# Output projection: the last block goes through DRAM and is split in its turn, x's rows and norm vectors load later, last attention normalisation on VectorE

## The chip, the cores and the metric

The kernel runs on one core of one Trainium2 chip. The metric is the device time of one execution in microseconds (us), as the median of several runs. A profile of one execution, with every engine's instructions, is read beside it. The engines are TensorE (PE; its weight loads are PEld), VectorE (DVE), ScalarE (ACT), GpSimd (POOL) and SyncE (SP), whose queue issues all the transfers of this kernel.

## The reference, cut to what matters

One decoder layer on x of 1024 positions by 1024 columns, all in float32. Four heads of differential attention (`o`, RMS-normalised per head) and a gated short convolution give two halves of 512 columns; they are put together and multiplied by `w_out`; then comes a layer norm over x plus that product, and a gated feed-forward with a second layer norm.

```python
o = o * lax.rsqrt(jnp.mean(jnp.square(o), axis=-1, keepdims=True) + RMS_EPS)
o = o * attn_norm_g.astype(jnp.float32) * (1.0 - lam_init)
...
conv_out = gate_b * causal_dwconv(gate_c * hc, conv_w)
cat = jnp.concatenate([attn_out, conv_out], axis=-1)
return jnp.einsum('bsc,cd->bsd', cat, w_out)
...
h = layer_norm(DEEPNORM_ALPHA * h + mix, ln1_g[l], ln1_b[l])
```

## The kernel before, in words

Every float32 product is made of three TensorE products of operands that are split in two parts, `hi` and `lo` (line 62, `split`: ScalarE copies the rounded part at line 65, VectorE subtracts it at line 66; `mm3`, lines 71 to 76, multiplies hi by hi, hi by lo, lo by hi).

Attention runs head after head, with the projections of the convolution's channel blocks between the heads (`CONV`). The last of these is `conv_3(2)`: `project` ends in a PSUM bank, `convolve(3)` (lines 467 to 473) makes three VectorE passes over 1024 positions, and `gate_out(3, ...)` multiplies the two halves by the gate at line 477, c0 (positions 0 to 511) first. The products of attention and convolution lie in DRAM as eight blocks of 128 channels, two halves of 512 positions each (`cat_d[k][half]`); blocks 0 to 3 are the heads, 4 to 7 the convolution. One piece is the exception: block 7, half 0, is not stored, but split out of `ws[3]` in SBUF, in a tile `c0_7` that is the first tile taken from the ring `e0` (seven tiles; lines 525 to 527). In the profile its two instructions are named `c<-w`.

The normalisation of an attention block (`normalise`, line 357) squares the block, sums it on TensorE against a matrix of ones (`mq`), takes the power on ScalarE (lines 368 to 371), and then does five steps of 128x256 on GpSimd (lines 372 to 376) and a store (line 377). The very last one, of head 3 and positions 768 to 1023, is called at line 519, behind all of attention and convolution.

The output projection goes over eight row tiles `t` of 128 positions; for each it sums over the eight blocks in `K_ORDER = (4, 5, 0, 1, 2, 6, 7, 3)`, position `i`. Rows 0 and 1 are made together: for each `i`, `weights(i)` loads and splits a row block of `w_out` (`wo`), `mixer(i, 0)` loads half 0 of a block (`cr`, four buffers) and splits it into a ring tile (`c<-cr`), and `mms(0, i)`, `mms(1, i)` make 12 matmuls (named `op`). At `i == 5` the loads of x's rows for tiles 0 and 1 (`rows`, tied behind the last `cr` load so far by `after`) and of the two norm vectors g1 and b1 are put in. Row tiles 2 to 7 follow with `norm` of earlier tiles and transposes (`trp`) between their matmuls.

The order of the instructions on each engine is the scheduler's: by the order in the code among what it holds to be ready. On the chip each engine's queue, and SP's queue of transfers, runs in that order and waits at its head.

Of the kernel before, what the change touches and what calls it, by code (L numbers as in the profile page):

```python
# [9 lines left out]
F32R = mybir.dt.float32r  # L10
BF16 = mybir.dt.bfloat16
AF = mybir.ActivationFunctionType
ALU = mybir.AluOpType
# [3 lines left out]
P = 128  # L17
S = 1024
D = 1024
NT = S // P  # L20
NK = D // P
H = 4
# [6 lines left out]
QC = 256  # L29
# [14 lines left out]
def layer_kernel(ctx: ExitStack, tc: tile.TileContext, x, xt, w_in, w_v, lam, vecs, w_out, ln, w_up, w_down, out):  # L44
    nc = tc.nc
    V, A, T, G = nc.vector, nc.scalar, nc.tensor, nc.gpsimd
    SQ = nc.sync
# [6 lines left out]
    def pool(name, stack=None, side=None, space=None, **kw):  # L54
        args = dict(name=name, bufs=1, reuse_waits="tile")
        if space is not None:
            args["space"] = space
        if side is not None:
            args["side"] = side
        return (stack or ctx).enter_context(tc.tile_pool(**args))  # L60

    def split(hi, lo, src, scale=None, eng=None):

        if scale is None:
            A.copy(hi, src)  # L65
            (eng or V).tensor_tensor(lo, src, hi.bitcast(F32), op=ALU.subtract)  # L66
        else:
            A.mul(hi, src, scale)
            V.scalar_tensor_tensor(lo, src, scale, hi.bitcast(F32), op0=ALU.mult, op1=ALU.subtract)
# [24 lines left out]
    RING = [6]  # L94
# [54 lines left out]
    cat_d = [[dram.tile([P, 512], F32, name=f"cat_d{k}_{c}") for c in range(2)] for k in range(8)]  # L149
# [156 lines left out]
    gm = const.tile([P, 1], F32, name="gm")  # L306
    V.tensor_scalar(gm, cols[:, 100:101], -0.5 * (1.0 - LAM_INIT), None, op0=ALU.mult)
    gp = const.tile([P, 1], F32, name="gp")
# [38 lines left out]
    c0, c1 = slice(0, 512), slice(512, 1024)  # L347
# [9 lines left out]
    def normalise(h, c, osb):  # L357
        sq = at.tile([P, QC], F32, name="sq", tag="sq")
        V.tensor_tensor(sq, osb, osb, op=ALU.mult)
        sqh = at.tile([P, QC], F32R, name="sqh", tag="sqh")  # L360
        sql = at.tile([P, QC], F32R, name="sql", tag="sql")
        split(sqh, sql, sq)
        mq = p_pv.tile([P, 512], F32, name="mq", tag="pv", bufs=1)
        T.matmul(mq[:, :QC], ones, sqh, start=True, stop=False)
        T.matmul(mq[:, :QC], ones, sql, start=False, stop=True)

        me = at.tile([P, QC], F32, name="me", tag="sq")
        A.activation(me, mq[:, :QC], AF.Identity, bias=epsc)
        y = at.tile([P, QC], F32, name="y", tag="sql")
        A.activation(y, me, AF.Ln)  # L370
        A.activation(y, y, AF.Exp, scale=-0.5)
        G.tensor_tensor(me, me, y, op=ALU.mult)
        G.tensor_tensor(me, me, y, op=ALU.mult)
        G.tensor_scalar(me, me, gm, gp, op0=ALU.mult, op1=ALU.add)
        G.tensor_tensor(y, y, me, op=ALU.mult)
        G.tensor_tensor(osb, y, osb, op=ALU.mult)
        SQ.dma_start(cat_d[h][c // 2][:, c % 2 * QC:(c % 2 + 1) * QC], osb)

    def attention(h):
# [28 lines left out]
        def spread(c, qi, pm, pa):  # L408
            i, nkb = 2 * c + qi, 2 * c + 2
            for j0 in range(0, i + 1, 4):  # L410
                nj = min(4, i + 1 - j0)
                tp = p_tr.tile([P, 4, P], F32, name="tp", tag="tr", bufs=1)
                for j in range(nj):
                    T.transpose(tp[:, j, :], pm[0][:, (j0 + j) * P:(j0 + j + 1) * P], ident)
                g = pa[j0 // 4]
                split(g[:, 0, 0:nj, qi * P:(qi + 1) * P], g[:, 1, 0:nj, qi * P:(qi + 1) * P], tp[:, :nj, :])
            if qi == 0:
                return
            o = p_pv.tile([P, 512], F32, name="o", tag="pv", bufs=1)
            for j in range(nkb):  # L420
                qs = slice(P if j == nkb - 1 else 0, QC)
                mm3(o[:, qs], vh[:, j, :], vl[:, j, :], pa[j // 4][:, 0, j % 4, qs], pa[j // 4][:, 1, j % 4, qs],
                    j == 0, j == nkb - 1, skip_group_check=True)
            osb = at.tile([P, QC], F32, name="osb", tag="osb")
            A.copy(osb, o[:, :QC])
            rms.append(lambda: normalise(h, c, osb))
# [48 lines left out]
    def gate_out(j, halves):  # L475
        for cs, v in halves:
            V.tensor_tensor(ws[j][:, cs], v, ws[j][:, cs], op=ALU.mult)
            if j < 3 or cs is c1:
                SQ.dma_start(cat_d[4 + j][cs.start // 512], ws[j][:, cs])

    us, ws = {}, {}

# [12 lines left out]
    def conv_2(j):  # L495

        ua, ub = new_u(j + 1)
        _, _, ba, bb = project(16 + j + 1, 12 + j, ua, ub)
        gate_out(j, ((c1, bb), (c0, ba)))

    def conv_3(j):

        va, vb, ba, bb = project(20 + j + 1, 12 + j + 1)
        ca, cb = us[j + 1][:, 2:514], us[j + 1][:, 514:S + 2]
        V.tensor_tensor(ca, va, ca, op=ALU.mult)
        V.tensor_tensor(cb, vb, cb, op=ALU.mult)
        convolve(j + 1)
        gate_out(j + 1, ((c0, ba), (c1, bb)))
# [14 lines left out]
    RING[0] = 7  # L523
    p8_st, hop_st, cp_st, d_st = ExitStack(), ExitStack(), ExitStack(), ExitStack()
    e0 = pool("e0", p8_st)
    cat = {(0, 7): e0.tile([P, 2, 512], F32R, name="c0_7", tag="ring", bufs=RING[0])}
    split(cat[0, 7][:, 0], cat[0, 7][:, 1], ws[3][:, c0])
    ab.close()
    p8 = pool("p8", p8_st, space=PSUM)
    ew = pool("ew", p8_st, side="right")  # L530
# [2 lines left out]
    gp = pool("gp", d_st)  # L533
# [19 lines left out]
    def bcast_row(pl, i, name):  # L553
        tl = pl.tile([P, D], F32, name=name, tag=name)
        SQ.dma_start(tl, ln[i:i + 1, :].broadcast_to([P, D]))
        return tl
# [30 lines left out]
    def weights(i):  # L587
        k = K_ORDER[i]
        raw = wtile([P, 2, 512], f"wo{k}_r")
        SQ.dma_start(raw, w_out[k * P:(k + 1) * P, :].rearrange("p (a b) -> p a b", a=2))  # L590
        w = late_p[i // 2].tile([P, 4, 512], F32R, name=f"wo{k}", tag=f"hb_{LATE_OPS[i // 2]}{'hl'[i % 2]}")
        split(w[:, 0:2], w[:, 2:4], raw)
        wo[k] = w

    def mixer(i, half):
        k = K_ORDER[i]
        if (half, k) in cat:
            return
        cr = cc.tile([P, 512], F32, name="cr", tag="cr", bufs=4)
        last_load[0] = SQ.dma_start(cr, cat_d[k][half])  # L600
        if i < NK - 1:
            c = e0.tile([P, 2, 512], F32R, name=f"c{half}_{k}", tag="ring", bufs=RING[0])
        else:
            c = cx.tile([P, 2, 512], F32R, name=f"c{half}_{k}", tag="c8")
        split(c[:, 0], c[:, 1], cr)
        cat[half, k] = c
# [3 lines left out]
    def rows(t):  # L610
        xr[t] = cx.tile([P, D], F32, name=f"xr{t}", tag="xr", bufs=5)
        d = SQ.dma_start(xr[t], x[t * P:(t + 1) * P, :])
        if t < 2:
            after(d, last_load[0])
# [4 lines left out]
    def mms(t, i):  # L619
        k = K_ORDER[i]  # L620
        c, w, ts = cat[t // 4, k], wo[k], slice(t % 4 * P, (t % 4 + 1) * P)
        for d in range(2):
            mm3(acc[t][d], c[:, 0, ts], c[:, 1, ts], w[:, d], w[:, 2 + d], i == 0, i == NK - 1)
# [61 lines left out]
    for i in range(NK):  # L685
        then.setdefault((3, i), []).append(lambda i=i: mixer(i, 1))
# [5 lines left out]
    for i in range(NK):  # L692
        weights(i)
        mixer(i, 0)
        if i == 5:
            for t in range(2):
                rows(t)
            g1, b1 = bcast_row(cp, 0, "g1"), bcast_row(cp, 1, "b1")
        for t in range(2):
            mms(t, i)  # L700
# [73 lines left out]
    def operand(src, which, i, tail=False, eng=None):  # L774
        if tail and not (which == "T" and i < HK - NTAIL + RT):
            v = ep.tile([P, 2, 512], F32R, name=f"{which}{i}", tag="ra", bufs=NF - NKEEP)
        else:
            v = e0.tile([P, 2, 512], F32R, name=f"{which}{i}", tag="ring", bufs=RING[0])
        split(v[:, 0, :], v[:, 1, :], src, eng=eng)
        return v  # L780
# [124 lines left out]
    def add(x_, y_, op, out=None):  # L905
        if out is None:
            out = ep.tile([P, 512], F32, name="tm", tag="r", bufs=4)
        V.tensor_tensor(out, x_, y_, op=op)
        return out
# [33 lines left out]
    for j in range(HK + 2):  # L943
        if j < HK:
            op = ready.pop(0) if ready else (operand(a11[j], "S", j), operand(b11[j], "T", j))
            for t in range(4):
                mm_row(X, op, t, j == 0, j == HK - 1)
        if j >= 2:
            i = j - 2
            op = (operand(add(a21[i], a22[i], ALU.add), "S", i),  # L950
                  operand(add(b12[i], b11[i], ALU.subtract), "T", i))
# [91 lines left out]
```

## Time and profile before

| | us |
|---|---|
| median of 3 runs (1127.42 to 1127.8) | 1127.51 |
| the profiled execution | 1126.14 |
| its span | 1124.4 |
| PE busy in the span | 1084.9 (96%) |
| DVE busy | 890.2 (79%) |
| ACT busy | 505.3 (45%) |
| POOL busy | 104.7 (9%) |

The span is the time from the first to the last instruction; the execution's own time lies 1.7 us above it. Busy shares are averages over stages with different limits, so the stage around the change, from 355 to 415 us, is read by itself.

### The profile page before, as it was taken

Reading aid. Unit: us, or ns where it says so; the run is one execution under the profiler, and the core shown is the slowest. Engines: PE = TensorE matmul, PEld = TensorE weight load, DVE = VectorE, ACT = ScalarE, POOL = GpSimd, SP = SyncE. Lnnn points to the kernel's source line nnn. Section 1 sums busy time; section 2 is a strip of 40 time slices with the busy share of each in tenths; the row PEclk is TensorE's granted clock in tenths of the full one; section 3 lists DMA queues with packets and bytes.
Section 4 is the critical chain, followed back from the end, with each engine's and each line's share of the span. In section 5 each row is a group of like instructions: output and inputs, shape, how many; then the busy total and the mean of one; then the engine's idle time right before and its main releaser. Section 6 shows DMA issues by size and latency. Waiting matters only on the chain.

```text
span 1124.4 us, 13769 instructions
## 1 busy us (share of the span) xinstructions
PE 1084.9 (96%) x4988; PEld 877.9 (78%) x4988; DVE 890.2 (79%) x1375; ACT 505.3 (45%) x936; POOL 104.7 (9%) x152
## 2 busy tenths in 40 slices
PE   7998999999999699999999999999999999999997
PEld 6877777877768588888888888888888887788885
DVE  7677799689787667898867677777777599997797
ACT  6367586387676311254333333343333343444550
POOL 0002214014032211100000000000000000000102
PEclk9999999999999899999999999999999999999998
DMA  7531201301214537022222222131312295111111
GB/s 268 151 94 43 77 33 48 113 28 48 80 48 147 210 135 272 38 90 98 87 101 75 94 71 99 60 109 57 113 57 94 85 380 219 38 66 38 42 71 76
DMA packets 48404, 113.80 MB, mean 101 GB/s; under 512 B 4816, under 2 KB 15184, under 8 KB 48336
## 3 DMA queue, kind: packets, MB, share of 16 engines
q1 hardware_dynamic: 48336, 112.92, 29.0%
q8 instruction: 39, 0.64, 0.2%
q14 instruction: 29, 0.24, 0.1%
HBM read 86.43 MB, written 26.48 MB: 100 GB/s over the span
## 4 chain that ended last, share of the span: by engine, by line
PE 76%; DVE 12%; ACT 5%; DMA 3%; POOL 2%; issue 2%; SPq 0%; POOLq 0%; DVEq 0%; ACTq 0%
PE X L74 9%; PE X L76 9%; PE X L75 9%; PE Z L76 5%; PE Z L74 5%; PE Z L75 5%; PE op L76 3%; PE op L74 3%; PE op L75 3%; PE dx L75 2%; PE dx L76 2%; PE dx L74 2%; PE Y L76 2%; PE dz L76 2%; PE dz L75 2%; PE Y L74 2%
## 5 line engine op out<-in xcount | busy, mean ns | idle before, releaser
L66 DVE TENSOR_TENSOR a<-s,a 128x512 fp32r<-128x512 f32 x118 | 85.4, 725 | 50.5 <-ACT a L65 49.6
L65 ACT CAST a<-s 128x512 fp32r<-128x512 f32 x118 | 73.6, 624 | 99.9 <-PE X L76 45.7
L65 ACT CAST a<-w 128x512 fp32r<-128x512 f32 x106 | 65.9, 623 | 97.2 <-PE X L76 40.8
L66 DVE TENSOR_TENSOR a<-w,a 128x512 fp32r<-128x512 f32 x106 | 74.1, 701 | 18.2 <-ACT a L65 17.9
L65 ACT CAST T<-b 128x512 fp32r<-128x512 f32 x66 | 40.6, 621 | 68.4 <-PE dz L76 34.0
L75 PE MATMUL dx<-T,S 128*128 128x512 f32 x176 | 69.1, 392 | 1.1 <-DVE T L66 1.1
L76 PE MATMUL dx<-T,S 128*128 128x512 f32 x176 | 68.6, 389 | 0.0
L74 PE MATMUL dx<-T,S 128*128 128x512 f32 x176 | 66.0, 390 | 0.0
L74 PE MATMUL op<-wo,c 128*128 128x512 f32 x128 | 51.5, 402 | 9.1 <-ACT c L65 9.1
L66 DVE TENSOR_TENSOR T<-b,T 128x512 fp32r<-128x512 f32 x66 | 46.0, 700 | 16.6 <-ACT T L65 16.4
L450 DVE TENSOR_REDUCE nm<-sc 128x1 f32<-128x128 f32 (+5 forms) x64 | 47.6, 751 | 6.2 <-PE sc L449 5.7
L75 PE MATMUL dz<-T,S 128*128 128x512 f32 x132 | 51.8, 393 | 0.0
L76 PE MATMUL dz<-T,S 128*128 128x512 f32 x132 | 51.4, 390 | 0.0
L76 PE MATMUL op<-wo,c 128*128 128x512 f32 x128 | 50.8, 397 | 0.2 <-DVE c L66 0.2
L75 PE MATMUL op<-wo,c 128*128 128x512 f32 x128 | 50.6, 396 | 0.0
L454 ACT ACTIVATE p<-sc,nm 128x128 f32<-128x128 f32 (+5 forms) x64 | 47.6, 745 | 6.2 <-DVE p L463 3.8
L74 PE MATMUL dz<-T,S 128*128 128x512 f32 x132 | 48.4, 394 | 0.5 <-ACT T L65 0.4
L813 ACT ACTIVATE t<-t 128x1024 f32<-128x1024 f32 x22 | 23.4, 1062 | 50.3 <-DVE t L812 50.3
L447 PE MATMUL sc<-k,q 128*128 128x512 f32 (+2 forms) x96 | 37.1, 394 | 5.6 <-ACT p L454 4.6
L75 PEld LDWEIGHTS dx<-T,S 128*128 128x128 f32 x176 | 33.0, 188 | 9.7 <-DVE T L66 2.9
L793 POOL MEMSET gs<- 128x2 f32 x22 | 2.2, 99 | 403.0 <-DVE t L812 403.0
L66 DVE TENSOR_TENSOR S<-ra,S 128x512 fp32r<-128x512 f32 x56 | 38.9, 698 | 0.0
(315 smaller groups left out, 3263.2 us busy)
## 6 DMA issues: line engine op xcount, KB each, us to landing
w<-in_w_up SPq DMA_DIRECT2D x44, 512.0 KB, 3.4
b<-in_w_down SPq DMA_DIRECT2D x44, 256.0 KB, 6.8
w<-in_w_in SPq DMA_DIRECT2D x20, 512.0 KB, 3.6
act_d<-act SPq DMA_DIRECT2D x19, 512.0 KB, 2.6
ra<-act_d SPq DMA_DIRECT2D x19, 512.0 KB, 7.5
v_d<-vs SPq DMA_DIRECT2D x16, 256.0 KB, 2.7
vhl<-v_d SPq DMA_DIRECT2D x8, 512.0 KB, 4.6
wo_r<-in_w_out SPq DMA_DIRECT2D x8, 512.0 KB, 3.9
```

The lines of the kernel that those rows point to most:

```text
L65: A.copy(hi, src)
L66: (eng or V).tensor_tensor(lo, src, hi.bitcast(F32), op=ALU.subtract)
L74: T.matmul(ps, lh, rh, start=first, stop=False, **kw)
L75: T.matmul(ps, lh, rl, start=False, stop=False, **kw)
L76: T.matmul(ps, ll, rh, start=False, stop=last, **kw)
L447: T.matmul(sc[:, bs], q2[m][:, qs], k2[m][:, bs], start=True, stop=False)
L450: V.tensor_reduce(nm[:, m:m + 1], sc[:, :n], axis=AX.X, op=ALU.max, negate=True)
L454: A.activation(pt[:, :n], sc[:, :n], AF.Exp, bias=nm[:, m:m + 1], accum_out=sm[:, m:m + 1])
L793: G.memset(gs[:, 0:2], 0.0)
L813: A.activation(t_, t_, AF.Silu)
```

## The change

Three edits. The last normalisation (head 3, last 256 positions) does its five steps on VectorE instead of GpSimd; the other fifteen stay. Half 0 of block 7 is stored to DRAM like all other pieces, and `c0_7` with its early split goes: `mixer(6, 0)` now loads the piece and splits it in its turn. The loads of x's rows 0 and 1 and of g1 and b1 are put in at `i == NK - 1` (7) instead of 5, so that the `after` of the rows refers to the load of block 3, the last one of half 0.

```diff
-        G.tensor_tensor(me, me, y, op=ALU.mult)
-        G.tensor_tensor(me, me, y, op=ALU.mult)
-        G.tensor_scalar(me, me, gm, gp, op0=ALU.mult, op1=ALU.add)
-        G.tensor_tensor(y, y, me, op=ALU.mult)
-        G.tensor_tensor(osb, y, osb, op=ALU.mult)
+        E = V if (h, c) == (H - 1, S // QC - 1) else G
+        E.tensor_tensor(me, me, y, op=ALU.mult)
+        E.tensor_tensor(me, me, y, op=ALU.mult)
+        E.tensor_scalar(me, me, gm, gp, op0=ALU.mult, op1=ALU.add)
+        E.tensor_tensor(y, y, me, op=ALU.mult)
+        E.tensor_tensor(osb, y, osb, op=ALU.mult)
...
-            if j < 3 or cs is c1:
-                SQ.dma_start(cat_d[4 + j][cs.start // 512], ws[j][:, cs])
+            SQ.dma_start(cat_d[4 + j][cs.start // 512], ws[j][:, cs])
...
-    cat = {(0, 7): e0.tile([P, 2, 512], F32R, name="c0_7", tag="ring", bufs=RING[0])}
-    split(cat[0, 7][:, 0], cat[0, 7][:, 1], ws[3][:, c0])
+    cat = {}
...
-        if (half, k) in cat:
-            return
...
-        if i == 5:
+        if i == NK - 1:
             for t in range(2):
                 rows(t)
             g1, b1 = bcast_row(cp, 0, "g1"), bcast_row(cp, 1, "b1")
```

## Rows read from the trace of the kernel before

**Rows 1.** Waits of PE, whole execution (us in total, times, longest).

```profile
PE op L74 <- ACT c L65: 9.1, 1, 9.1
```

**Rows 2.** Waits of PE from 385 us to the end.

```profile
PE dx L75 <- DVE T L66: 1.1, 2, 0.9
PE dz L74 <- ACT T L65: 0.4, 1, 0.4
```

**Rows 3.** Timeline of PE around the stage (start, us, engine, line, operation).

```profile
370.52 0.28 PE L365 MATMUL mq<-sql,ones 128*128 128x256 f32 x1
379.90 0.79 PE L74 MATMUL op<-wo,c 128*128 128x512 f32 x1 [9.10 <-ACT c L65]
...
384.44 0.39 PE L74 MATMUL op<-wo,c 128*128 128x512 f32 x1
...
385.83 0.40 PE L74 MATMUL op<-wo,c 128*128 128x512 f32 x1
...
412.45 1.03 PE L574 MATMUL trp<-ident,xr 128*128 128x128 f32 x8
```

**Rows 4.** Busy time by stretch: length, PE, PEld, DVE, ACT, POOL, PEclk, DMA share, GB/s.

```profile
380.00:385.00 5.00, 4.83 (x12) 3.35 (x13) 3.04 (x5) 1.41 (x3) 0.08 (x1) 0.56 0.78 199
```

**Rows 5.** Timeline of ACT from 360 us.

```profile
372.16 0.42 ACT L371 ACTIVATE y<-y 128x256 f32<-128x256 f32 x1
378.71 0.62 ACT L65 CAST c<-w 128x512 fp32r<-128x512 f32 x1 [6.13 <-DVE w L477]
379.23 2.17 ACT L65 CAST c<-cr 128x512 fp32r<-128x512 f32 x4
```

**Rows 6.** Timeline of SP, the transfer queue, from 318 us.

```profile
339.95 1.35 SPq L600 DMA_DIRECT2D cr<-cat_d  x3
...
381.46 0.91 SPq L600 DMA_DIRECT2D cr<-cat_d  x2
382.41 0.99 SPq L612 DMA_DIRECT2D xr<-in_x  x2
```

**Rows 7.** Landing of all 15 loads of `cr`, then of `xr`, 375 to 405.

```profile
DMA to landing us min/median/max: 2.7/4.3/8.8
...
DMA to landing us min/median/max: 4.7/8.0/9.8
```

**Rows 8.** Timeline of DVE from 318 us.

```profile
357.68 0.69 DVE L66 TENSOR_TENSOR a<-w,a 128x512 fp32r<-128x512 f32 x1 [1.99 <-ACT a L65]
...
372.13 1.22 DVE L66 TENSOR_TENSOR wo<-wo_r,wo 128x1024 fp32r<-128x1024 f32 x1
...
374.94 1.74 DVE L66 TENSOR_TENSOR wo<-wo_r,wo 128x1024 fp32r<-128x1024 f32 x1
...
377.98 0.69 DVE L477 TENSOR_TENSOR w<-X,w 128x512 f32<-128x512 f32 x1
378.59 0.91 DVE L477 TENSOR_TENSOR w<-p,w 128x512 f32<-128x512 f32 x1
...
380.56 2.49 DVE L66 TENSOR_TENSOR c<-cr,c 128x512 fp32r<-128x512 f32 x4
...
407.96 1.27 DVE L569 SCALAR_TENSOR_TENSOR xr<-xr,rs,b 128x1024 f32<-128x1024 f32 x1
```

**Rows 9.** Transfers, 360 to 400 us, then 325 to 360: count, KB, us to landing.

```profile
cat_d<-w SPq DMA_DIRECT2D x1, 256.0 KB, 2.2
...
cat_d<-w SPq DMA_DIRECT2D x2, 256.0 KB, 4.9
```

**Rows 10.** Instructions of lines 471 and 359 (count, min/median/max ns, first and last start).

```profile
L471 DVE SCALAR_TENSOR_TENSOR w<-u,cols,w x4: 1271/1462/1751, 126.7 to 373.3; 128x1024 f32<-128x1024 f32 x4
L359 DVE TENSOR_TENSOR sq<-osb x16: 416/422/426, 89.9 to 354.3; 128x256 f32<-128x256 f32 x16
```

**Rows 11.** PE by stretch around its wait of 3.50 us (PE, PEclk, DMA share, GB/s).

```profile
104.00:106.00 2.00, 1.27 (x4) 0.64 0.05 18
106.00:108.00 2.00, 2.00 (x7) 0.51 0.00 0
```

## The prediction

> **What bounds the kernel now.** I read the waits of PE first. Over the whole execution the longest is one wait of 9.1 us of the first matmul of the output projection, for ScalarE's copy `c` [rows 1]; it is the stage that the change touches. From 385 us on PE waits for only 1.1 + 0.4 = 1.5 us in 739 [rows 2], so PE sets the time there, and what is saved before that point should reach the end in full.
>
> The timeline of PE shows the price of this stall. The last matmul before it starts at 370.52; its pair started 0.12 earlier, so PE could go on at about 370.7. The first `op` starts at 379.90, and after that PE runs slowly: from 379.90 to 384.44 are nine steps in 4.54 us, later six steps take 384.44 to 385.83, 0.23 each [rows 3]. Nine steps at 0.23 would be 2.1. So 2.4 us more are lost, and the granted clock says to what: 0.56 over 380 to 385, the lower of the two levels (1.2 GHz of 2.4) for most of it [rows 4]. The stage costs 9.1 + 2.4 = 11.5 us in all.
>
> Then the releaser. ScalarE is done with the last normalisation at 372.6, then idles 6.13 us for the convolution's gate (line 477) before `c<-w`, the split of block 7 out of SBUF; the four `c<-cr` come right behind [rows 5]. These four had been loaded long before: SP issued the first three of their loads from 339.95 to 341.3 [rows 6], and no `cr` load of the execution took over 8.8 us [rows 7]. Their data was there, and they stood behind one copy. PE's first matmul needs one of these four (block 4), not block 7, which it wants only at `i` = 6. The eight splits of `wo` ran before `c<-w` although the code asks for them later, so the order was not the code's alone. I infer that the ring gives its tiles in the order asked, and that `c0_7`, which asks first, holds the four.
>
> **The change part by part.** *The early split goes.* The ring's first tile is then block 4's. It lies where operands of the finished projection lay, so the four splits can go as soon as ScalarE and VectorE have room: VectorE waited 1.99 us before 357.68 alone [rows 8], and a split's lower half costs it 2.49 / 4 = 0.62. PE has `wo` and `c` of the first blocks when it is done with `mq`, and starts at 370.7: it gains 9.1. As it does not pause, it gains the 2.4 of the slow clock too. Were the splits done only in VectorE's full stretch behind 361 us, they would still be ahead of what PE asks: one `wo` and one `c` are 1.22 + 0.62 = 1.84 us of VectorE [rows 8] against 12 matmuls, 2.8 us of PE. With their buffers free early, the loads of blocks 2 and 6, which SP issued only at 381.46 [rows 6], leave early too.
>
> *Block 7 through DRAM.* This adds a store, a load and a later split. Call D the end of the first gate product of line 477; before it is 378.6 [rows 8]. PE asks for block 7 after six positions, 72 matmuls: 370.7 + 72 x 0.231 = 387.3. Behind D come 0.1 for the issue, the store's landing, which SP's queue must wait for, the load's landing, and 0.6 for ScalarE's half of the split; the lower half ends 0.7 later and is wanted 0.46 later, so 0.8 in all. The store took 2.2 us beside other transfers in this stage and 4.9 earlier [rows 9]; the load from 2.7 to 8.8, in the middle 4.3 [rows 7]. I take 2.2, since it was measured in this place, and 4.3, since g1 and b1 (512 KB each) will be in flight with it as g1 and the rows were before.
>
> *The last normalisation on VectorE.* Five steps of the size of line 359, 0.42 each at most [rows 10], add up to 2.1 us on VectorE, and may stand ahead of the gate product or behind it. In return GpSimd no longer disturbs VectorE there: the `wo` split at 374.94 took 1.74 against 1.22 [rows 8], line 471 took 1.75 against 1.27 [rows 10]; D falls by 0.5 + 0.5 = 1.0 to 377.6. If the five steps and the lower halves of blocks 2 and 6 (1.2) all come ahead, D is 380.9. I take 379.0, about half. Block 7 is then ready for PE at 379.0 + 0.1 + 2.2 + 4.3 + 0.8 = 386.4, which is 0.9 before it is wanted: hidden, cost 0. The bounds: at best 377.6 + 0.1 + 2.2 + 2.7 + 0.8 = 383.4, at worst 380.9 + 0.1 + 4.9 + 8.8 + 0.8 = 395.5, a wait of 8.2 us. The store of the normalised block stands in SP's queue ahead of the two stores of `w`; it can hold them up by the five steps at most, which D's upper bound has.
>
> A rule speaks against a round trip like this one. The Trainium skill, DMA: Bandwidth & Descriptors, section Anatomy of one DMA, gives each transfer about 2.0 us that don't shrink with its size, plus its bytes at 436 GB/s (fitted on transfers that GpSimd issues); an estimate from it is 2.6 us for 256 KB, 5.2 for store and load. The rows say 2.2 + 4.3 = 6.5 for the same two. By the page block 7 would come 1.3 us earlier than by the rows and the sum would be the same; the upper rows, 4.9 + 8.8, are what it leaves out, and they carry the second rival.
>
> *Rows of x and norm vectors later.* Four loads of 512 KB are moved, all in SP's queue, from behind block 6's load to behind block 3's. g1 and b1 may slip ahead again, as nothing ties them; the 4.3 above has them in flight. The two rows are issued behind block 3's load, some 0.5 us after block 7's, near 382.5, where the rows were issued before as well (382.41) [rows 6]. Loads of rows landed in 8.0 us in the middle and 9.8 at most [rows 7]: 390.5 to 392.3. Tile 0's sums end at about 370.7 + 90 x 0.231 = 391.5. Before, the last step of its norm ended at 409.23 [rows 8] and PE's transposes that need it started at 412.45 without a wait [rows 3]: 3.2 us of cover. The cost is 0.
>
> **Sum.** 9.1 + 2.4 - 0 = 11.5 us. The profiled execution would go from 1126.14 to 1114.6; the median of the runs lies 1.37 above that execution, so 1127.51 becomes 1116.0.
>
> **The rivals.** *Block 7 comes late.* PE stalls at `i` = 6. For it: the load's landing runs up to 8.8 and VectorE is full there; against it: the middle values leave 0.9. With a wait of 2 to 8.2 us the gain is 9.5 down to 3.3. A wait of 3.50 us elsewhere was followed by a clock of 0.64 and 0.51 in the next two stretches of 2 us [rows 11], (1 - 0.64) x 2 + (1 - 0.51) x 2 = 1.7 us lost; so the longer waits lose 1.7 to 2.4 more, and the gain is down to 0.9: 1118 to 1126.6.
>
> *The four splits stay late.* Something other than `c0_7` orders them, and they stand behind the gate product as before. Only `c<-w` (0.62) and GpSimd's disturbance (1.0) leave the chain, and up to 2.1 of normalisation enter it: between 1.6 faster and 0.5 slower, 1126 to 1128. Against it: the data lay there for 30 us, and ScalarE idled.
>
> *Slower: x's rows come too late.* They now queue behind a load that waits for a store. The place is tile 0's norm, the first transposes wait on it in PE's order. It costs from a landing at 391.5 + 3.2 = 394.7 on, and turns the change into a loss of 0.2% only from 394.7 + 11.5 + 2.3 = 408.5 on, 26 us after the issue, where 9.8 was the longest [rows 7]. A queue entry put ahead of them that waits for something late could do it; nothing in the rows shows one.
>
> **How the numbers follow.** About 0.2%, 2.3 us, is what a measurement of this kernel can tell from no change. The forecast (wait under 2 us) has 0.70; block 7 late 0.18, three quarters of it with more than 2.3 us left; the splits stay late 0.07; slower 0.05. Faster is then 0.70 + 0.14, and 0.02 more for the part of the third case near its best end: 0.86; same 0.09; slower 0.05. The range starts at 1114.0, 2 below the forecast, for PE waits before 370 that the new order could fill, and reaches to 1122.5, a late block 7 that costs 6.5; outside lie about 0.18.
>
> **What would show it.** Right: PE's wait before the first `op` is gone, the granted clock stays at 1.00 over 370 to 385, four `c<-cr` stand before 371 on ScalarE, GpSimd has no work there, and `op` runs to the end of tile 1 without a wait over 1 us. Wrong: a wait of `op` for ScalarE's `c` near 387 (late block 7); the `c<-cr` still behind line 477; a wait of `trp` for VectorE after 400; or any wait of PE behind 385 us that adds up to more than the 1.5 us of now, which would give the gain back.

## The result, and the profile after

The median went from 1127.47 to 1115.47 us; the ratio is 0.9896 with a 95% interval of 0.9879 to 0.9913, that is 12.0 us less, between 9.8 and 13.6. The profiled execution of the changed kernel took 1116.29 us, with a span of 1114.5. Lines behind the first edit have moved by one to three: 372 to 376 are 373 to 377 now, 477 is 478, 574 is 573.

The first view of the changed kernel is the timeline of PE around the stage; it answers to [rows 3].

```profile
372.50 0.28 PE L365 MATMUL mq<-sql,ones 128*128 128x256 f32 x1
372.63 0.39 PE L74 MATMUL op<-wo,c 128*128 128x512 f32 x1
...
402.64 1.03 PE L573 MATMUL trp<-ident,xr 128*128 128x128 f32 x8
```

The first `op` follows `mq` without a wait. From the last `mq` to the first transposes were 412.45 - 370.52 = 41.9 us, and are 402.64 - 372.50 = 30.1 now: the stage is 11.8 us shorter. The stage begins 2.0 us later than in the profile of before, since PE waited 2.3 us for its second operand at the start of this execution (0.6 before). That wait differs between executions of one kernel: a second profile of the changed kernel has 1.1 there, and its stage is 30.1 us long as well.

The busy time by stretch answers to [rows 4] (length, PE, PEld, DVE, ACT, POOL, PEclk, DMA share, GB/s).

```profile
371.00:380.00 9.00, 9.00 (x42) 7.47 (x41) 8.60 (x13) 3.11 (x5) 0.00 (x0) 1.00 0.25 93
380.00:385.00 5.00, 5.00 (x24) 4.15 (x23) 3.94 (x6) 0.99 (x2) 0.00 (x0) 1.00 0.66 219
```

PE is busy throughout, the granted clock is 1.00, and GpSimd (the fifth pair) does nothing. ScalarE's timeline answers to [rows 5].

```profile
359.53 2.18 ACT L65 CAST c<-cr 128x512 fp32r<-128x512 f32 x4
...
365.51 1.14 ACT L65 CAST c<-cr 128x512 fp32r<-128x512 f32 x2
...
373.78 0.42 ACT L371 ACTIVATE y<-y 128x256 f32<-128x256 f32 x1
...
383.99 1.25 ACT L65 CAST c<-cr 128x512 fp32r<-128x512 f32 x2 [8.71 <-DMA cr<-cat_d]
```

The four splits that stood behind `c<-w` at 379 run at 359.5, and the next two, blocks 2 and 6, at 365.5. The last pair are block 7 and block 3; ScalarE waits 8.7 us for their loads, VectorE then waits 1.1 us for ScalarE, and PE waits for neither. VectorE and SP's queue around block 7 answer to [rows 8] and [rows 6].

```profile
377.30 0.41 DVE L375 TENSOR_SCALAR me<-me,gm,gp 128x256 f32<-128x256 f32 x1
377.63 0.68 DVE L478 TENSOR_TENSOR w<-X,w 128x512 f32<-128x512 f32 x1
378.23 0.68 DVE L478 TENSOR_TENSOR w<-p,w 128x512 f32<-128x512 f32 x1
...
384.65 1.33 DVE L66 TENSOR_TENSOR c<-cr,c 128x512 fp32r<-128x512 f32 x2 [1.06 <-ACT c L65]
```

```profile
378.34 0.93 SPq L479 DMA_DIRECT2D cat_d<-w  x2
380.74 0.32 SPq L378 DMA_DIRECT2D cat_d<-osb  x1
381.15 1.35 SPq L597 DMA_DIRECT2D cr<-cat_d  x3
382.60 0.85 SPq L609 DMA_DIRECT2D xr<-in_x  x2
383.50 0.43 SPq L554 DMA_DIRECT2D g<-in_ln  x1
```

The first gate product ends at 378.3 and its store leaves at once; the normalised block's store comes behind it now, and then the loads, rows and norm vectors last. Block 7 is ready at about 385.3, and PE reaches it, with its 73rd `op`, at 389.0. Behind 376 us PE's waits are those of [rows 2], 1.6 us in all. The second profile of the same kernel has one more: a `trp` of a later row tile waits 0.8 us at 427 for VectorE's norm.

### The profile page after: what moved, and what is told of

It is laid out like the page before. It is cut to its first block, busy times and chain, and to the rows that moved or that the text cites. A ratio compares the mean times of both kernels' runs of the same rounds, so it can differ in the third digit from the quotient of the medians.

```text
span 1114.5 us, 13774 instructions
## 1 busy us (share of the span) xinstructions
PE 1082.9 (97%) x4988; PEld 877.4 (79%) x4988; DVE 890.1 (80%) x1380; ACT 504.7 (45%) x936; POOL 98.7 (9%) x147
## 4 chain that ended last, share of the span: by engine, by line
PE 77%; DVE 11%; ACT 4%; DMA 3%; POOL 2%; issue 2%; SPq 0%; POOLq 0%; DVEq 0%; ACTq 0%
PE X L76 9%; PE X L74 9%; PE X L75 9%; PE Z L76 5%; PE Z L74 5%; PE Z L75 5%; PE op L75 3%; PE op L74 3%; PE op L76 3%; PE dx L75 3%; PE dx L76 2%; PE dx L74 2%; PE Y L74 2%; PE Y L76 2%; PE dz L74 2%; PE dz L76 2%
## 5 line engine op out<-in xcount | busy, mean ns | idle before, releaser
L74 PE MATMUL op<-wo,c 128*128 128x512 f32 x128 | 50.6, 395 | 0.0
L76 PE MATMUL op<-wo,c 128*128 128x512 f32 x128 | 50.0, 390 | 0.0
L75 PE MATMUL op<-wo,c 128*128 128x512 f32 x128 | 50.0, 390 | 0.0
L75 PEld LDWEIGHTS dx<-T,S 128*128 128x128 f32 x176 | 33.0, 188 | 9.7 <-DVE T L66 2.9
L74 PEld LDWEIGHTS dx<-T,S 128*128 128x128 f32 x176 | 33.0, 188 | 7.4 <-ACT T L65 0.6
L76 PEld LDWEIGHTS dx<-T,S 128*128 128x128 f32 x176 | 33.1, 188 | 6.7
```

The costliest lines, as they stand in the source:

```text
L74: T.matmul(ps, lh, rh, start=first, stop=False, **kw)
L75: T.matmul(ps, lh, rl, start=False, stop=False, **kw)
L76: T.matmul(ps, ll, rh, start=False, stop=last, **kw)
```

## The experiments

The theory to test: the ring gives its tiles in the order of their first use, so the early split of block 7 held the other splits and with them PE; the round trip is one way out of that order, and the other two edits matter only as far as they keep block 7's way short. The rivals: the normalisation on VectorE made the gain, or the late loads, or the price of the stage is not what the waits and the clock say.

**Block 7 through DRAM alone.** The changed kernel with

```diff
-        E = V if (h, c) == (H - 1, S // QC - 1) else G
+        E = G
...
-        if i == NK - 1:
+        if i == 5:
```

> Block 7 through DRAM alone; the last normalisation stays on GpSimd and x's rows and the norm vectors keep their place. Theory (the early split held the ring, the other two edits only guard block 7's way): the 9.1 us wait before the first op is gone, but SP's queue now has the normalised block's store, which waits some 7 us for GpSimd, and two loads of x's rows ahead of the two stores of block 7. Block 7 reaches PE some 3 to 5 us after it is asked for at position 6, the clock falls with it: 1119 to 1123 us. Rival (the edits are worth what they are worth by themselves, and block 7's alone gives the whole): 1115 to 1116.5. Rival (VectorE's normalisation made the gain): 1126 to 1128.

Measured 1122.38, ratio 0.9955 (0.994 to 0.997): 4.8 us of the 12 by the medians, 5.1 by the ratio. The wait of `op` and the timeline of SP in this run, whose last `mq` starts at 371.64 (372.50 in the changed kernel):

```profile
PE op L74 <- ACT c L65: 5.9, 1, 5.9
```

```profile
381.29 0.33 SPq L378 DMA_DIRECT2D cat_d<-osb  x1
381.67 0.92 SPq L609 DMA_DIRECT2D xr<-in_x  x2
382.68 0.86 SPq L479 DMA_DIRECT2D cat_d<-w  x2
383.64 0.86 SPq L554 DMA_DIRECT2D g<-in_ln  x1
384.54 0.74 SPq L554 DMA_DIRECT2D b<-in_ln  x1
388.56 0.80 SPq L597 DMA_DIRECT2D cr<-cat_d  x2
```

The wait of 9.1 us is gone, and one of 5.9 has come, now at position 6. Block 7's stores leave 11.0 us behind the last `mq` instead of 5.8. Half of that delay is VectorE's: the gate product ends at 380.1, 8.4 us behind `mq` instead of 5.8. The other half, 2.6 us, is the queue's, where the normalised block's store and two row loads stand ahead. The stores took 5.9 us to land beside 2 MB of loads (2.1 in the changed kernel), so block 7's load left at 388.6.

**The other two edits without it.** The kernel before, with the last normalisation on VectorE and rows and norm vectors asked for at position 7; block 7 stays as it was.

> The other two edits without block 7's: the last normalisation on VectorE, rows and norm vectors late, block 7 still split early out of SBUF. Theory: the wait before the first op stays, since the four splits still stand behind the early one; GpSimd's disturbance of VectorE goes (1.0 us) and five steps come in (up to 2.1): 1125.9 to 1128.0, a wait of 7.5 to 10 us. Rival (GpSimd's normalisation and the queue it held made the stall): 1115 to 1120.

Measured 1125.54, ratio 0.9985 (0.9976 to 0.9994). The wait stays:

```profile
379.57 0.80 PE L74 MATMUL op<-wo,c 128*128 128x512 f32 x1 [7.53 <-ACT c L65]
```

1.6 us are won (0.7 to 2.7 by the interval); the median lies 0.4 below the range that was expected. The wait is shorter by the same 1.6: the gate product ends 6.6 us behind the last `mq` instead of 8.2. About 1.0 of that is VectorE undisturbed by GpSimd, as expected; the rest is order, since a split of `wo` now stands behind the gate product and only two short steps came ahead of it. The two edits together don't make the gain.

**The normalisation back on GpSimd.** The changed kernel with `E = G`.

> The changed kernel with the last normalisation back on GpSimd. Theory: its store stands ahead of block 7's stores in SP's queue and holds them until GpSimd is done, about 7 us after the exponential; block 7's load leaves 3 us later than in the changed kernel and comes 0 to 2 us too late: 1115.5 to 1118. By the prediction (the store can hold them up by no more than the five steps) and by the rival (only the ring's order counts): 1115 to 1116, no wait of op over 0.5 us.

Measured 1116.47, ratio 0.9903 (0.9888 to 0.9918), which overlaps the changed kernel's; the profile shows the difference. PE, VectorE and SP in this run, whose last `mq` starts at 371.65:

```profile
389.12 0.50 PE L74 MATMUL op<-wo,c 128*128 128x512 f32 x1 [0.85 <-ACT c L65]
```

```profile
374.03 1.76 DVE L472 SCALAR_TENSOR_TENSOR w<-u,cols,w 128x1024 f32<-128x1024 f32 x1
...
379.40 0.68 DVE L478 TENSOR_TENSOR w<-X,w 128x512 f32<-128x512 f32 x1
```

```profile
381.30 0.33 SPq L378 DMA_DIRECT2D cat_d<-osb  x1
381.68 0.91 SPq L479 DMA_DIRECT2D cat_d<-w  x2
382.69 0.41 SPq L554 DMA_DIRECT2D g<-in_ln  x1
383.81 0.80 SPq L597 DMA_DIRECT2D cr<-cat_d  x2
```

Block 7's stores leave 10.0 us behind the last `mq` instead of 5.8, and the queue is the smaller part of these 4.2 us. 2.6 are VectorE's: the gate product ends at 380.1, 8.4 us behind `mq` instead of 5.8. Two splits of `wo` and one of `c` stand ahead of it, where three short steps stand in the changed kernel, and instructions beside GpSimd's steps are longer (line 472 took 1.76 us, and 1.28 in the changed kernel). The other 1.6 are the queue's: the normalised block's store waits for GpSimd until 381.3, with block 7's stores behind it. Then block 7's load takes 4.6 us, beside other loads, instead of 2.8. The spare time in front of position 6 is used up, and PE waits 0.85 us.

**The loads back at position 5.** The changed kernel with `if i == 5:`.

> The changed kernel with x's rows 0 and 1 and the norm vectors asked for at position 5 again. Theory: nothing, 1115 to 1116, no wait of op; their transfers leave in the same places of SP's queue, behind block 7's load. Rival (the late loads keep the transfers free for block 7): they run beside block 7's load, which lands 2 to 4 us later: up to 1118.

Measured 1115.77, ratio 0.9892 (0.9876 to 0.9909), no wait of `op`: this edit is worth nothing that can be told where the normalisation is on VectorE. Where it is on GpSimd it is worth 1122.38 - 1116.47 = 5.9 us (the first and the third run), since it is then that two row loads slip in ahead of block 7's stores. The two edits are two guards of one thing.

**No round trip at all.** The kernel before, with a tile of its own for block 7's early split; x's rows give up one of five buffers for the space.

```diff
-    cat = {(0, 7): e0.tile([P, 2, 512], F32R, name="c0_7", tag="ring", bufs=RING[0])}
+    cat = {(0, 7): e0.tile([P, 2, 512], F32R, name="c0_7", tag="c07", bufs=1)}
...
-        xr[t] = cx.tile([P, D], F32, name=f"xr{t}", tag="xr", bufs=5)
+        xr[t] = cx.tile([P, D], F32, name=f"xr{t}", tag="xr", bufs=4)
```

> The kernel before with one thing different: block 7's half 0 is split out of SBUF as before, but into a tile of its own instead of the ring's first; to make room, x's rows have four buffers instead of five. No round trip through DRAM. Theory (the ring gives its tiles in the order of their first use, and the early one holds the rest): the four splits run before 371 us, no wait before the first op, 1115 to 1117, as the changed kernel. Rival (the piece must leave ScalarE's queue, or the wait for the gate product is what counts): the wait of some 9 us stays, 1126 to 1128. Rival (four row buffers cost): between, with a wait of op or trp after 400 us.

Measured 1115.59, ratio 0.9902 (0.9881 to 0.9922). ScalarE in this run:

```profile
359.20 2.19 ACT L65 CAST c<-cr 128x512 fp32r<-128x512 f32 x4
...
380.42 0.62 ACT L65 CAST c<-w 128x512 fp32r<-128x512 f32 x1 [4.10 <-DVE w L477]
```

`c<-w` waits for the gate product as it always did, now behind everything that PE needs sooner. So it was the place in the ring that cost, and DRAM is not needed for the gain, nor are the other two edits. Four row buffers instead of five show no price: PE's waits behind 376 us are 1.5 us in all. By what rule the ring lets a late first tile hold the others no trace shows; the order of first use stays an inference.

**The wait filled.** The kernel before, with 36 matmuls of 128x512 put behind the last `mq`; their sums are read by nobody.

```diff
+        if i == 0:
+            wd = bank("wd")
+            for _ in range(36):
+                after(T.matmul(wd, wo[4][:, 0, 0:P], wo[4][:, 0], start=True, stop=True, skip_group_check=True), last_mq[0])
```

> The kernel before with 36 additional matmuls of 128x512 behind the last mq, whose sums nobody reads: they fill some 8.4 of the 9.1 us in which PE waits. The wait for the four splits is as before. Theory (2.4 us of the stage's 11.5 are the lower clock after the wait): the granted clock stays at 1.00 over 380 to 385, the first op starts at the same time, and 1.5 to 2.4 us are saved: 1125 to 1126. Rival (PE is slow there because splits come one by one): no gain, 1127 to 1128, or more where the filling delays the first op.

Measured 1125.73, ratio 0.9986 (0.9974 to 0.9997). PE in this run:

```profile
372.23 0.28 PE L365 MATMUL mq<-sql,ones 128*128 128x256 f32 x1
372.35 8.33 PE L697 MATMUL wd<-wo 128*128 128x512 f32 x36
380.94 0.50 PE L74 MATMUL op<-wo,c 128*128 128x512 f32 x1 [0.26 <-ACT c L65]
381.29 0.39 PE L75 MATMUL op<-wo,c 128*128 128x512 f32 x1
382.43 0.50 PE L76 MATMUL op<-wo,c 128*128 128x512 f32 x1 [0.75 <-DVE c L66]
```

The granted clock is 1.00 over 380 to 385 (0.56 before). The first ten `op` take 3.2 us from start to start (380.94 to 384.15) instead of 4.5, so 1.3 us of the 2.4 come back; most of the rest turns into a wait for VectorE's half of the split (0.75). VectorE takes 3.57 us for the four halves here, and 2.49 before [rows 8], so 1.3 is the least that the clock costs. Another 0.7 us is from `op` starting 8.7 us after `mq` instead of 9.4, which was not expected to move.

**Block 7 wanted sooner.** The changed kernel with `K_ORDER = (4, 5, 0, 7, 1, 2, 6, 3)`.

> The changed kernel with block 7 summed fourth instead of seventh (order 4, 5, 0, 7, 1, 2, 6, 3). PE asks for it at about 372.6 + 36 x 0.231 = 380.9, and in the changed kernel it is ready at 384.6 to 385.3. Theory (the round trip costs nothing only while six positions of matmuls cover it): a wait of 3 to 4.5 us at the fourth position and 1.5 to 2 of lower clock behind it: 1119.5 to 1122. Rival (the order of the sums is free, the round trip is short): 1115 to 1116.5.

Measured 1121.37, ratio 0.9947 (0.993 to 0.9965), some 5.8 us above the changed kernel.

```profile
383.28 0.80 PE L74 MATMUL op<-wo,c 128*128 128x512 f32 x1 [3.57 <-ACT c L65]
```

A wait of 3.57 us at the fourth position, with a granted clock of 0.81 over 380 to 385 and 0.85 over 385 to 390, that is (0.19 + 0.15) x 5 = 1.7 us more: 5.3 in all. The round trip is free only behind enough matmuls.

**The same cause elsewhere.** PE's wait of 3.50 us near 104 [rows 11] is in the changed kernel too. ScalarE's copy of an attention block waits there for the one buffer `osb`, which a late GpSimd normalisation holds until its store has landed. In the changed kernel:

```profile
103.66 0.37 ACT L426 COPY osb<-o 128x256 f32<-128x256 f32 x1 [3.37 <-DMA cat_d<-osb]
```

Three runs take the changed kernel with one, two and three of head 0's normalisations on VectorE as well. The edit of the third is:

```diff
-        E = V if (h, c) == (H - 1, S // QC - 1) else G
+        E = V if (h, c) in ((0, 0), (0, 1), (0, 2), (H - 1, S // QC - 1)) else G
```

> The changed kernel with a second normalisation on VectorE, that of head 0, positions 0 to 255. In the changed kernel GpSimd ends it late; its store frees the one buffer of the attention block, ScalarE waits 3.4 us for it and PE 3.5 us near 102, with the lower clock behind. Theory (a late GpSimd normalisation costs PE there what it waits, 3.5 and 1.5 of clock, less what five steps take from VectorE in attention): 1110 to 1114, the wait under 1.5 us. Rival (VectorE is the bound in attention, the steps push its own chain): 1115 to 1117.5.

> The changed kernel with two more normalisations on VectorE, head 0 at positions 0 to 255 and 256 to 511. With the first alone, PE's 3.5 us wait near 102 went and a wait of 2.7 us near 117 came, behind ScalarE's 4.1 us for the store of the second. Theory (each late GpSimd normalisation holds the one buffer of the next block): the 2.7 us and their clock go too, less what five more steps take: 1109.5 to 1113. Rival (VectorE's own chain is the bound by now): 1112.5 to 1115.

> As the run with three, and the third normalisation of head 0 on VectorE too. Theory: nothing more to win unless PE waits for its store; within 1 us of the run with three, and slower rather than faster, since VectorE has the steps to do: 1110 to 1114. Rival (every one on VectorE gains): 1107 to 1110.

> The changed kernel itself on this chip, to set the two runs beside it: 1115 to 1116.5, and a ratio to the kernel before of 0.988 to 0.991.

| on VectorE | median us | ratio to before | 95% interval |
|---|---|---|---|
| head 3's last (changed kernel, second time) | 1115.52 | 0.9893 | 0.9878 to 0.9907 |
| and head 0's first | 1113.13 | 0.988 | 0.9859 to 0.9901 |
| and head 0's second | 1110.66 | 0.985 | 0.9834 to 0.9867 |
| and head 0's third | 1109.53 | 0.9841 | 0.9826 to 0.9855 |

PE's stretches (PE, PEclk, DMA share, GB/s) in the changed kernel, then in the run with three in all:

```profile
100.00:110.00 10.00, 6.51 (x25) 0.74 0.19 66
110.00:120.00 10.00, 9.81 (x54) 0.92 0.05 16
```

```profile
100.00:110.00 10.00, 10.00 (x58) 1.00 0.19 68
110.00:120.00 10.00, 9.80 (x51) 1.00 0.04 13
```

With the first alone the wait moved to the second block: PE waited 2.7 us at 117, ScalarE 4.1 for that block's store. With both, PE is full from 100 to 110 at the full clock. The last two rows beat the changed kernel clearly; between themselves their intervals overlap, so whether the third is worth its steps stays open. It was expected at 1110 to 1114 and rather slower; its 1109.53 lies below that range, in the rival's (every one on VectorE gains).

## Why the prediction was right

- *What bounds, and the sum of 11.5.* From event to event the stage gave back 11.8 us, and the medians 12.0. The wait and the slow clock were both gone, as the granted 1.00 and the missing wait show. As separate prices they are less clean than the sum: with the clock held up and the wait kept, 1.3 of the 2.4 came back and most of the rest was waiting for splits again, so the clock's own price lies between 1.3 and 2.4.
- *The ring's order.* It was inferred from an order on ScalarE. A tile of its own for the early split gives the same gain with no round trip, which shows that its place in the ring was the cause; the rule behind it stays inferred.
- *Block 7 hidden.* Right, with 3.7 us to spare instead of 0.9, but the working was off, and that it was off to the good side was luck. The gate product ended 1.3 us below the lower bound for D: 378.3 less the 2.0 by which this stage starts later is 376.3, against 377.6 at best. The bound took VectorE's order as it was. Three splits of `wo`, which stood ahead of the gate product before, went behind it, and three of the five steps came ahead. Store and load took 2.1 and 2.8 us, where 2.2 and 4.3 were taken. The estimate of 5.2 for the two, from the Trainium skill (DMA: Bandwidth & Descriptors, section Anatomy of one DMA), fits here, and doesn't fit the 5.9 + 4.9 of the run in which 2 MB of loads were in flight with them.
- *The normalisation on VectorE.* The term that was mis-sized, though the forecast didn't suffer. It was priced by VectorE's time alone, up to 2.1 us against 1.0, with its store ahead of block 7's for the length of its steps at most. Beside the run with it on GpSimd, this edit lets the gate product end 2.6 us sooner and frees SP's queue 1.6 us sooner. Without it PE waits 0.85 us, or 5.9 where rows slip in as well. And the normalised block's store stands behind block 7's stores now, not ahead; it holds the loads instead, by 0.7 us (the first store has landed at 380.4, block 7's load leaves at 381.15).
- *Rows and norm vectors later: 0.* Right for the kernel as changed, and right only there. A wait of `trp` for VectorE after 400 was named as a sign of being wrong: one of the two profiles of the changed kernel has one, of 0.8 us and of a later row tile, the other none, and the two medians agree (1115.47 and 1115.52).

## What to carry to other kernels

When an engine's queue stands still, ask which instruction is at its head and why it got there: here one late piece that had the first tile of a buffer ring made all behind it wait, and a tile of its own cured that for one row buffer. A load or store that waits in an in-order transfer queue charges its wait to whatever is queued behind it, so price an edit by the queue it stands in as well as by its engine. Work that moves to another engine can change the order of that engine's queue too: here the gate product came 2.6 us sooner although VectorE had five steps more to do. Two edits can guard the same weak place; taken out one at a time, each seems worth little or nothing.

## What the runs showed of the hardware

The five steps of 128x256 on GpSimd took 7.4 us from first to last in the profile of before (372.65 to 380.09), and 3.9 us at another place of it (335.66 to 339.51, at most 0.74 a step). On VectorE they took 0.42 each at most, spread between other work. The Trainium skill (SBUF — State Buffer, section Who interferes with whom) has GpSimd and VectorE contend for a read port where VectorE reads two operands from SBUF, which fits the run with the normalisation back on GpSimd: four of its steps took 1.3 to 1.9 us beside VectorE's two-operand instructions, and VectorE's line 472 took 1.76 instead of 1.28. No run here isolates the port.

A store of 256 KB landed in 2.1 us with little beside it, and in 5.9 with four loads of 512 KB issued around it. And a wait of PE of 3.6 us cost 1.7 us of lower clock behind it, nearly half as much again.
